# Gates' low-rank path moved beside the second group's recurrence, and a triangular inverse put together from 16x16 blocks, in a streaming-encoder trunk

## The chip, the cores and the metric

The kernel runs on one core of a Trainium2 chip. The metric is the device time of one execution in microseconds. The kernel before takes 1319.26 us, the median of 3 runs (1318.08 to 1319.82). One execution was recorded by the hardware profiler; all rows below come from it.

## The reference

The trunk has four residual layers on a 512 x 1024 activation (one batch): a spatial-gating MLP, a gated convolutional FFN, an RWKV-7 time mixer and a second FFN, each behind an RMS norm, and a last norm. Only the RWKV layer is changed:

```python
xx = token_shift(h) - h                      # h: 512 x 1024, already normed
xr, xw, xk, xv, xa, xg = (h + xx * mu[i] for i in range(6))
r, k, v = xr @ w_r, xk @ w_k, xv @ w_v
w = -softplus(-(w0 + tanh(xw @ w1) @ w2)) - 0.5      # w1: 1024 x 64
a = sigmoid(a0 + (xa @ a1) @ a2)                     # a1: 1024 x 64
g = sigmoid(xg @ g1) @ g2                            # g1: 1024 x 160, g2: 160 x 1024
...                                                  # kk from k; 16 heads of 64
y = wkv7_scan(r, exp(-exp(w)), k, v, -kk, kk * a)    # delta-rule state per head
y = groupnorm(y) * ln_w + ln_b + bonus               # bonus: sum(r*k*r_k) * v
return (y * g) @ w_o
```

The kernel doesn't step through 512 tokens. It cuts them into 8 chunks of 64; inside a chunk the recurrence becomes products of 64 x 64 matrices, one of which is the inverse of a unit triangular matrix per head and chunk.

## The kernel before, in words

**Layout and arithmetic.** Activations lie transposed: 8 k-tiles of 128 features by 512 tokens. Every large product is made in three parts from operands that are split into a high and a low half (`mm3`, L280: high·high, high·low, low·high). A split (`split`, L204) is a copy on ScalarE (the high half, L212) and a subtraction on VectorE or POOL (L213).

**The RWKV layer** has 16 heads in two groups of 8. It goes through these stages:

- `rwkv_first` (L621): low-rank products for decay and `a` on the incoming operand, not yet normed; the shift and the norm are made up for afterwards by `shifted` (L645), which needs `rb`, the norm's factor broadcast to all partitions (`rstd`, L313). Then the gate's low-rank products `ga` and `gb`, in the same way (weights scaled on VectorE, L371, then split; 72 parts of products), then the projection by `wra`, for which each k-tile is normed (L671), mixed (`mix`, L610: L612 on ScalarE, L613 on VectorE) and split into `mxh` and `mxl`. The gate's values go through tanh, are split and go out to memory (`sgd`). Last the projection by `wrb`.
- `pairs` (L915) with `projections` (L742): head pairs make the chunk matrices, while projections of k and v fill TensorE. `value` (L784) centres v (L790) and makes the bonus (L804). `invert(0)` (L942) runs beside the last pairs.
- `scan(0)` (L1036): the 8 chunks of group 0, each a chain of small products and copies (L1066, L1070, L1079, L1086, L1091), where the next chunk needs the state written by L1089. `vu` is the state and value operand, `us` and `e` are accumulators; L1081 is a copy on ScalarE that belongs to the chain. Beside it run the rest of the projections and `invert(1)`.
- `scan(1)` with `project` (L1144), the output projection by `wo`. `finish` (L1102) normalizes each pair of chunks (L1110 to L1120) and every second time gates the result (`mm3` and L1133 on 256 tokens, then L1135 to L1139). The gate values `sg` and weights `gw` are loaded at chunk 1 of each group (`gate_weights`, L1004).

**The inverse.** `invert` treats the 32 x 32 diagonal blocks of the 64 x 64 triangular matrices of a group, 128 of them, by forward substitution on VectorE: 31 steps of a multiplication (L970) and an addition (L971), then a transposition (L976). The two blocks of a matrix are put together by two products for each (L991, L994), in plain float32, which the trace shows as two passes each, addressed to 32 x 32 tiles of TensorE's array.

**What sets the order.** Programs are generators. `weave` (L1225) advances a main one (pairs or a scan), now and then a side one (the inverse), and a filling one (projections or the output projection) by rates in `RATES`; `LEAD` is a number of filling steps ahead of `scan(0)`. Each engine then works through its own queue in that order. Loads of weights are issued from ScalarE's queue (`wq`), loads of chunks and of the residual `h` from SP's.

Of the kernel before, what the change touches and what calls it, by code (L numbers as in the profile page):

```python
# [19 lines left out]
P = 128  # L20
# [10 lines left out]
RATES = ((1.9, 2), (1.9, 6, 2.2), (0.8, 2, 2), (0.7, 2), (2, 2), (0.7, 6, 2.2))  # L31
LEAD = 6
# [21 lines left out]
COFF = dict(ident=0, bones=128, center=256, masks=384, smask=512, causal=1024, blk2=1152, one=1154, id2=1155)  # L54
NCST = 1219


def constants():
# [13 lines left out]
    c[:, 1155:1219] = (i % C)[:, None] == np.arange(C)[None, :]  # L72
    return c


def layout(inp):
# [34 lines left out]
    a["g1a"] = g1[:, :, :P].reshape(P, 1024)  # L111
    a["g1b"] = np.concatenate([g1[:, :, P:], g1[:, :, P:]], axis=2).reshape(P, 512)
# [31 lines left out]
class Emit:  # L144
    def __init__(self, ctx, tc, A, out):
# [24 lines left out]
        self.wd = {n: [dp.tile([P, 2, 1024], F32, name=f"{n}d{m}") for m in range(KT)] for n in PARTS}  # L170
        self.n = self.turn = 0
# [69 lines left out]
    def make_parts(self, pool):  # L241

        nc = self.nc
        at = [(n, m, slice(c, c + 512)) for n in PARTS for m in range(KT) for c in (0, 512)]
        w = []
        for i in range(len(at) + 1):
            with self.tc.issue_after(self.last(mybir.EngineType.Activation)):
                if i < len(at):
                    n, m, c = at[i]
                    w.append(pool.tile([P, 512], F32, tag="pw", bufs=2, name=self.uid("pw")))  # L250
                    nc.sync.dma_start(w[i], self.A[n][m][:, c])
                if i:
                    n, m, c = at[i - 1]
                    for j, x in enumerate(self.split(pool, w[i - 1], [P, 512], "pw", bufs=1)):
                        nc.sync.dma_start(self.wd[n][m][:, j, c], x.bitcast(F32))
            yield

    def parts(self, n, m, whole):
# [13 lines left out]
        return 512, t  # L272

# [310 lines left out]
    def rwkv(self, gain):  # L584
        nc, tc, A = self.nc, self.tc, self.A
        V, S, G = nc.vector, nc.scalar, nc.gpsimd
        with ExitStack() as ctx:
# [7 lines left out]
            r.sgd = dp.tile([3, P, T], F32, name="sgd")  # L595
# [12 lines left out]
            def mix(i, k):  # L608
# [5 lines left out]
                return self.operand(t, lo_eng=(G, V)[k % 2])  # L614
# [6 lines left out]
    def rwkv_first(self, r, ep):  # L621
# [5 lines left out]
        r.sg = [ep.tile([P, T], F32R, name=f"sg{i}") for i in range(3)]  # L627

# [3 lines left out]
        def lowrank(n, w):  # L632
            a = self.acc()
            self.dense(a[0:n], w, hx, ncol=n)
            return a[0:n]
# [9 lines left out]
        def shifted(now, before, n):  # L645
            t, u = tmp("lt", 2), tmp("lu", 2, T + 1)
            G.memset(u[:, 0:1], 0.0)
            V.tensor_tensor(t[0:n], now, rb[0:n], ALU.mult)
            V.tensor_tensor(u[0:n, 1:], before, rb[0:n], ALU.mult)
            G.tensor_tensor(t[0:n], t[0:n], u[0:n, 0:T], ALU.add)  # L650
            return t
# [4 lines left out]
        S.activation(t[0:64], t[0:64], AF.Tanh)  # L656

        for j, x in enumerate(r.lr):
            hi, lo = slice(64 * j, 64 * j + 64), slice(64 - 64 * j, 128 - 64 * j)
            S.copy(x[hi], t[hi])  # L660
            V.tensor_tensor(x[lo], t[hi], x[hi].bitcast(F32), ALU.subtract)
# [4 lines left out]
        for kk in range(4):  # L666
            w = self.weights(A["wra"][kk])
            for j in range(2):
# [10 lines left out]
        for i, (x, n) in enumerate(((ga, P), ((gb[0:32], gb[32:64]), 32))):  # L679
            t = shifted(*x, n)[0:n]  # L680
            S.activation(t, t, AF.Tanh, scale=0.5)
            V.tensor_scalar(t, t, 0.5, 0.5, ALU.mult, ALU.add)
            if i == 0:
                S.copy(r.sg[0], t)
                V.tensor_tensor(r.sg[1], t, r.sg[0].bitcast(F32), ALU.subtract)
            else:
                self.stack(r.sg[2], t)
        for i, n in enumerate((P, P, 96)):
            nc.sync.dma_start(r.sgd[i, 0:n], r.sg[i][0:n].bitcast(F32))
# [13 lines left out]
    def rwkv_main(self, r, ctx, gain):  # L703
# [38 lines left out]
        def projections():  # L742

            load = Ahead([lambda n=n, m=m: self.parts(n, m, m % 3 == 2) for n in PARTS for m in range(KT)])
# [197 lines left out]
        def invert(g):  # L942
# [11 lines left out]
            pr = ip.tile([P, 272], F32, tag="pr", bufs=1, name=self.uid("pr"))  # L954
# [7 lines left out]
            V.transpose(li.rearrange("p s t -> p t s"), x.rearrange("p u t -> p t u"))  # L962
            for _ in range(WAIT):
                yield
            for j in range(31):
                ni, nj = 31 - j, j + 1
                a = li[:, j, j + 1:32].unsqueeze(1).to_broadcast([P, nj, ni])
                b = tt[:, 0:nj, j].unsqueeze(2).to_broadcast([P, nj, ni])
                q = pr[:, 0:ni * nj].rearrange("p (c i) -> p c i", i=ni)
                V.tensor_tensor(q, a, b, ALU.mult)  # L970
                V.tensor_tensor(tt[:, 0:nj, j + 1:32], tt[:, 0:nj, j + 1:32], q, ALU.add)  # L971
# [311 lines left out]
```

## Time and profile before

| what | value |
|---|---|
| median of 3 runs | 1319.26 us (1318.08 to 1319.82) |
| profiled execution | 1317.32 us, span 1315.5, mean granted clock 0.978 |
| `rwkv_first` | 519.35 to 593.88 us |
| pairs, projections, group 0's inverse | 593.88 to 772.32 us |
| `scan(0)`, group 1's inverse, the last projections | 772.32 to 839.19 us |
| `scan(1)`, output projection, the first products of the last FFN | 839.19 to 941.09 us |
| instructions | 19526 |

Times in rows are us from the start of the span. A row of the timeline has start, duration, engine, line, operation, output<-inputs, shape, count and, in brackets, idle time before it with what ended it. A matmul row's duration is longer than the distance to the next, since they are pipelined; the distance of starts is its cost in a row of many. The granted clock is a fraction of full speed.

### The profile page before, as it was taken

What the parts mean: (1) busy time and instruction counts of PE and PEld (TensorE: products, weight loads), DVE (VectorE), ACT (ScalarE), POOL (GpSimd) and SP (SyncE); (2) the same over time, 40 slices, a digit from 0 to 9 for tenths busy, and PEclk for the clock granted to TensorE, in tenths of its full rate; (3) what the DMA queues carried; (4) which work ended last, traced back from release to release, by engine and by line L of the source; (5) the groups of instructions that cost most, each with busy time, mean ns of one, the idle gap of its engine ahead of it and who ended that gap; (6) DMA issues with size and microseconds to landing.
All of it is one profiled execution on the core that took longest, in us unless ns stands there. A gap on an engine that the chain in (4) does not pass through costs nothing.

```text
span 1315.5 us, 19526 instructions
## 1 busy us (share of the span) xinstructions
PE 1272.7 (97%) x7618; PEld 1031.3 (78%) x7618; DVE 848.5 (64%) x1365; ACT 623.8 (47%) x1062; POOL 142.8 (11%) x152
## 2 busy tenths in 40 slices
PE   8999999999999999999999998898999999999996
PEld 6878888888888888787777766676888888888886
DVE  5565488788874444865869785656687777772223
ACT  5444455555554333565657644333554444442221
POOL 3100200000000010310111012332300000000001
PEclk9999999999999999999979996999999999999998
DMA  7332345555556753245877786881333232333322
GB/s 259 88 113 80 106 151 170 167 168 174 166 173 211 224 150 108 79 136 157 251 220 205 225 209 147 207 221 41 96 96 97 96 96 96 97 92 91 101 89 76
DMA packets 100461, 188.55 MB, mean 143 GB/s; under 512 B 16912, under 2 KB 47760, under 8 KB 100368
## 3 DMA queue, kind: packets, MB, share of 16 engines
q10 hardware_dynamic: 36448, 109.46, 27.2%
q1 hardware_dynamic: 63920, 77.84, 20.7%
q8 instruction: 60, 0.98, 0.3%
q14 instruction: 33, 0.27, 0.1%
HBM read 146.70 MB, written 40.57 MB: 142 GB/s over the span
## 4 chain that ended last, share of the span: by engine, by line
PE 78%; DVE 9%; ACT 3%; issue 2%; DMA 2%; POOL 1%; ACTq 0%; DVEq 0%; SPq 0%; POOLq 0%
PE mm L284 8%; PE mm L285 8%; PE mm L286 8%; PE e L284 5%; PE e L286 5%; PE e L285 5%; PE us L284 5%; PE us L286 5%; PE us L285 5%; PE aux L284 5%; PE aux L286 5%; PE aux L285 5%; DVE tt L971 1%; DVE pr L970 1%; PE us L1066 1%
## 5 line engine op out<-in xcount | busy, mean ns | idle before, releaser
L212 ACT CAST wh<-w 128x512 fp32r<-128x512 f32 (+1 forms) x361 | 220.1, 612 | 398.8 <-PE mm L285 97.1
L213 DVE TENSOR_TENSOR wl<-w,wh 128x512 fp32r<-128x512 f32 x353 | 243.8, 692 | 186.9 <-ACT wh L212 182.8
L284 PE MATMUL mm<-mxh,wh 128*128 128x512 f32 x392 | 161.2, 412 | 0.6 <-DVE h L1166 0.4
L285 PE MATMUL mm<-mxl,wh 128*128 128x512 f32 x392 | 155.7, 397 | 0.6 <-DVE mxl L1139 0.6
L286 PE MATMUL mm<-mxh,wl 128*128 128x512 f32 x392 | 155.9, 398 | 0.3 <-DVE wl L213 0.3
L311 POOL TENSOR_TENSOR ss<-ss,sq 128x512 f32<-128x512 f32 x30 | 40.7, 1357 | 777.3 <-issue 594.8
L284 PEld LDWEIGHTS mm<-mxh,wh 128*128 128x128 f32 x392 | 74.8, 191 | 20.1 <-issue 3.2
L507 ACT ACTIVATE cv<-z,par 128x512 f32<-128x512 f32 x88 | 71.7, 817 | 36.0 <-DVE z L505 35.9
L286 PEld LDWEIGHTS mm<-mxh,wl 128*128 128x128 f32 x392 | 74.7, 191 | 17.3 <-DVE wl L213 0.6
L285 PEld LDWEIGHTS mm<-mxl,wh 128*128 128x128 f32 x392 | 74.8, 191 | 16.3 <-DVE mxl L1139 1.3
L284 PE MATMUL e<-mxh,wh 128*128 128x512 f32 x216 | 84.5, 391 | 0.0
L284 PE MATMUL us<-mxh,wh 128*128 128x512 f32 (+1 forms) x216 | 84.4, 391 | 0.0
L286 PE MATMUL us<-mxh,wl 128*128 128x512 f32 (+1 forms) x216 | 84.1, 389 | 0.0
L285 PE MATMUL us<-mxl,wh 128*128 128x512 f32 (+1 forms) x216 | 84.1, 389 | 0.0
L285 PE MATMUL e<-mxl,wh 128*128 128x512 f32 x216 | 84.0, 389 | 0.0
L286 PE MATMUL e<-mxh,wl 128*128 128x512 f32 x216 | 84.0, 389 | 0.0
L508 DVE SCALAR_TENSOR_TENSOR cv<-z,par,cv 128x512 f32<-128x512 f32 x88 | 66.1, 752 | 23.9 <-ACT cv L507 23.9
L284 PE MATMUL aux<-mxh,wh 128*128 128x512 f32 x208 | 81.2, 391 | 0.2 <-ACT wh L212 0.2
L286 PE MATMUL aux<-mxh,wl 128*128 128x512 f32 x208 | 81.1, 390 | 0.0
L285 PE MATMUL aux<-mxl,wh 128*128 128x512 f32 x208 | 80.9, 389 | 0.0
L509 DVE SCALAR_TENSOR_TENSOR cv<-z,par,cv 128x512 f32<-128x512 f32 x88 | 66.0, 752 | 2.9
L284 PEld LDWEIGHTS e<-mxh,wh 128*128 128x128 f32 x216 | 40.6, 188 | 8.7 <-issue 0.5
(1071 smaller groups left out, 2679.4 us busy)
## 6 DMA issues: line engine op xcount, KB each, us to landing
w<-in_wup ACTq DMA_DIRECT2D x88, 512.0 KB, 3.5
w<-in_wdn ACTq DMA_DIRECT2D x32, 512.0 KB, 3.6
st<-std SPq DMA_DIRECT2D x32, 384.0 KB, 5.8
std<-lq SPq DMA_DIRECT2D x32, 256.0 KB, 4.6
w<-in_wdn ACTq DMA_DIRECT2D x16, 384.0 KB, 3.3
w<-in_wsu ACTq DMA_DIRECT2D x8, 512.0 KB, 3.5
w<-in_wso ACTq DMA_DIRECT2D x8, 512.0 KB, 3.5
pw<-in_wk SPq DMA_DIRECT2D x16, 256.0 KB, 3.9
```

The source lines that it names most:

```text
L212: nc.scalar.copy(hi[r, :n], src)
L213: (lo_eng or nc.vector).tensor_tensor(lo[r, :n], src, hi[r, :n].bitcast(F32), ALU.subtract)
L284: mm(acc, wh, xh, start=first, stop=False)
L285: mm(acc, wh, xl, start=False, stop=False)
L286: mm(acc, wl, xh, start=False, stop=last)
L311: nc.gpsimd.tensor_tensor(self.ss, self.ss, self.sq, ALU.add)
L507: nc.scalar.activation(c, z[:, 2:], AF.Identity, scale=cw(2, i), bias=self.p("conv_b", l * 44 + i))
L508: nc.vector.scalar_tensor_tensor(c, z[:, 1:T + 1], cw(1, i), c, ALU.mult, ALU.add)
L509: nc.vector.scalar_tensor_tensor(c, z[:, 0:T], cw(0, i), c, ALU.mult, ALU.add)
L970: V.tensor_tensor(q, a, b, ALU.mult)
L971: V.tensor_tensor(tt[:, 0:nj, j + 1:32], tt[:, 0:nj, j + 1:32], q, ALU.add)
L1066: nc.tensor.matmul(us[H[hd], 0, i, :], ar(i, hd, 0), vu[:, hd, i, :], start=True, stop=True)
```

## The change

Three things are done.

1. **The gate's low-rank path.** Its 72 partial products leave `rwkv_first`, with the scaling of weights, the shift and the trip to memory and back. A new generator `gates` runs in front of `project` as the filling work of `scan(1)`: it mixes and splits each k-tile of the normed input, multiplies by `g1` (48 partial products, 6 a k-tile), makes tanh and the splits, then gates all of group 0 in pieces of 512 tokens. The halves of `g1` are made beside the first FFN (`make_parts`) and lie in memory (`gd`). `h`, which `project` reloads with the residual, now stays the normed input until `gates` is through.
2. **The inverse.** Substitution goes down to 16 x 16 diagonal blocks: 15 steps, two blocks in one operation. Three rounds of products, 32 x 16 each (128, 64 and 128 of them in an inverse), put 32 x 32 blocks together; the 64 x 64 assembly stays.
3. **Order.** New `RATES`, `LEAD` 3 for 6; `scan(0)` no longer waits for the fourth `value` before it begins, but its loads do (`load`). In `rwkv_first` the norm's broadcast stands after 30 products instead of 48, with the low-rank results taken up after the second weight, and the mixes' low halves alternate between VectorE and POOL the other way round.

```diff
-RATES = ((1.9, 2), (1.9, 6, 2.2), (0.8, 2, 2), (0.7, 2), (2, 2), (0.7, 6, 2.2))
-LEAD = 6
+RATES = ((1.9, 2), (1.9, 6, 1.7), (0.65, 2, 1), (0.9, 2), (2, 2), (0.7, 6, 2))
+LEAD = 3
...
+        at += [(self.A["g1"], self.gd, slice(c, min(c + 512, 1280))) for c in (0, 512, 1024)]
...
-                return self.operand(t, lo_eng=(G, V)[k % 2])
+                return self.operand(t, lo_eng=(V, G)[k % 2])
...
-        lw = [lowrank(P, self.first)]
+        lw = [self.acc() for _ in range(2)]
+        self.dense(lw[0], self.first, hx[:4], last=False)
         norm = self.rstd()
         next(norm)
-        lw.append(lowrank(P, w))
+        self.dense(lw[0], self.first, hx[4:], first=False, c0=4 * P)
+        self.dense(lw[1], w, hx[:2], last=False)
         rb = next(norm)
+        self.dense(lw[1], w, hx[2:], first=False, c0=2 * P)
...
-        ga = [lowrank(P, self.lowrank_weights(A["g1a"], P, [f[:, :, 5]])) for f in (om, mu)]
-        gb = lowrank(64, self.lowrank_weights(A["g1b"], 64, [om[:, :, 5], mu[:, :, 5]]))
-        t = shifted(*lw, P)
...
+            if kk == 1:
+                lowrank()
...
-            for j in range(31):
-                ni, nj = 31 - j, j + 1
-                a = li[:, j, j + 1:32].unsqueeze(1).to_broadcast([P, nj, ni])
-                b = tt[:, 0:nj, j].unsqueeze(2).to_broadcast([P, nj, ni])
-                q = pr[:, 0:ni * nj].rearrange("p (c i) -> p c i", i=ni)
+            for j in range(15):
+                ni, nj = 15 - j, j + 1
+                a = diag(li, j, j + 1, [0, nj], [1, ni])
+                b = diag(tt, 0, j, [32, nj], [0, ni])
+                o = diag(tt, 0, j + 1, [32, nj], [1, ni])
+                q = pr[:, 0:2 * ni * nj].rearrange("p (d c i) -> p d c i", d=2, i=ni)
                 V.tensor_tensor(q, a, b, ALU.mult)
-                V.tensor_tensor(tt[:, 0:nj, j + 1:32], tt[:, 0:nj, j + 1:32], q, ALU.add)
+                V.tensor_tensor(o, o, q, ALU.add)
...
+            def small(out, lhs, rhs, rows):
+                for n in range(32):
+                    for r0 in rows:
+                        nc.tensor.matmul(out[r0, n, :], lhs(r0, n), rhs(r0, n), start=True, stop=True,
+                                         tile_position=(r0.start, r0.start))
...
+            small(q, lambda r0, n: tg[r0, n, col[r0.start]], lambda r0, n: z[r0, n, 0:16], quads)
+            V.tensor_tensor(w[:, :, 0:16], q, id4[:, :, 0:16].to_broadcast([P, 32, 16]), ALU.add)
+            yield
+            q = bank()
+            small(q, lambda r0, n: y[r0, n, :], lambda r0, n: w[r0, n, 0:16], firsts)
+            for r0 in firsts:
+                S.copy(z[r0, :, 0:16], q[r0])
+            yield
+            q = bank()
+            small(q, lambda r0, n: w[r0, n, :], lambda r0, n: y[r0, n, 16:32], quads)
+            S.copy(y[:, :, 16:32], q)
+            yield
...
+        def gates():
+            gw[0] = gate_weights(0)
+            ws = self.gate_parts()
+            yield
+            accs = [self.acc("mm")[0:n] for n in (P, 32)]
+            for k in range(KT):
...
+                    S.activation(t, self.hz[k][:, 0:T], AF.Copy, scale=self.p("mu", j))
+                    V.scalar_tensor_tensor(t, self.h[k], self.omu[:, j:j + 1], t, ALU.mult, ALU.add)
+                    x = self.operand(t)
+                for a, w, n in zip(accs, ws, (P, 32)):
+                    self.mm3(a, self.wcols(w, k * n, n), x, k == 0, k == KT - 1)
+                yield
...
+            while 0 not in normed:
+                yield
+            for i in range(4):
+                gate(0, i, slice(0, T))
+                yield
+            gated.add(0)
+            gw[1] = gate_weights(1)
...
         def load(g, c):
+            while 4 * g + 3 not in vdone:
+                next(fill)
...
-        while 3 not in vdone:
-            next(fill)
...
-        fill = project()
+        fill = itertools.chain(gates(), project())
```

The order in which an engine gets its work is not to be read from this. Three places follow; a row has a line, an operation, output<-inputs and a shape, with the line numbers of the kernel it stands in.

VectorE at the start of `rwkv_first`, before (`h_66` to `h_69` are k-tiles of the activation, `rb` the norm's broadcast, `w` and `wl` weights, `mt` a mix, `mxl` its low half):

```order
L213 TENSOR_TENSOR wl_4468<-w_861_4460,wh_4467 128x512
L213 TENSOR_TENSOR wl_4500<-w_867_4496,wh_4499 128x512
L371 TENSOR_TENSOR w_873_4532<-w_873_4532,omu 128x8x32
L371 TENSOR_TENSOR w_873_4532<-w_873_4532,par 128x8x32
L213 TENSOR_TENSOR wl_4504<-w_867_4496,wh_4503 128x512
L648 TENSOR_TENSOR lt_4565<-aux_4390,rb_4458 128x512
L649 TENSOR_TENSOR lu_4566<-us_4428,rb_4458 128x512
L671 SCALAR_TENSOR_TENSOR h_66<-h_66,par,rb_4458 128x512
L671 SCALAR_TENSOR_TENSOR h_67<-h_67,par,rb_4458 128x512
```

And with the change:

```order
L215 TENSOR_TENSOR wl_4488<-w_874_4485,wh_4487 128x512
L215 TENSOR_TENSOR wl_4492<-w_874_4485,wh_4491 128x512
L673 SCALAR_TENSOR_TENSOR h_66<-h_66,par,rb_4461 128x512
L673 SCALAR_TENSOR_TENSOR h_67<-h_67,par,rb_4461 128x512
L215 TENSOR_TENSOR wl_4540<-w_885_4537,wh_4539 128x512
L624 SCALAR_TENSOR_TENSOR mt_4497<-h_66,omu,mt_4497 128x512
L624 SCALAR_TENSOR_TENSOR mt_4518<-h_67,omu,mt_4518 128x512
L673 SCALAR_TENSOR_TENSOR h_68<-h_68,par,rb_4461 128x512
L215 TENSOR_TENSOR mxl_4501<-mt_4497,mxh_4500 128x512
```

The gate's weight scaling (L371) and the shift (L648, L649) no longer stand ahead of the normed k-tiles; the first mixes stand among the first weight splits.

TensorE in `scan(0)` where group 1's inverse is put together, before (L991 and L994 are the assembly of 64 x 64, L790 and L804 work of `value`, the others a chunk's chain):

```order
L804 MATMUL mm_7290<-rt_4363,wb_7288 128x512
L1086 MATMUL us_7114<-vu_6976,cbt_6975 64x64 x8
L1091 MATMUL e_7115<-vu_6976,st_6974 64x64 x8
L991 MATMUL aux_7218<-ix_7175,ti_5021 32x32 x32
L991 MATMUL aux_7253<-ix_7175,ti_5021 32x32 x32
L1066 MATMUL us_7302<-vu_7107,st_7105 64x64
L1070 MATMUL e_7303<-vu_7107,st_7105 64x64
L1066 MATMUL us_7302<-vu_7107,st_7105 64x64 x7
L1070 MATMUL e_7303<-vu_7107,st_7105 64x64 x7
```

With the change, a little earlier in the program (L987 is the new small product, L296 to L298 are `mm3`, L1145 to L1170 the chain):

```order
L987 MATMUL aux_7318<-ix_7282,ti_4913 32x16 x128
L785 MATMUL mm_7556<-cst,v_7286 128x128 x4
L1145 MATMUL us_7456<-vu_7222,st_7220 64x64
L1149 MATMUL e_7457<-vu_7222,st_7220 64x64
L296 MATMUL mm_7288<-mxh_5585,wh_7080 128x512
L1145 MATMUL us_7456<-vu_7222,st_7220 64x64 x7
L1149 MATMUL e_7457<-vu_7222,st_7220 64x64 x7
L1196 MATMUL aux_7479<-cst,y_7035 128x128 x4
L987 MATMUL aux_7488<-tt_7316,li_7283 32x16 x64
L297 MATMUL mm_7288<-mxl_5586,wh_7080 128x512
L298 MATMUL mm_7288<-mxh_5585,wl_7081 128x512
```

Between the chain's products now stand blocks of 128, 64 and 128 small products, and between these, parts of projections.

ScalarE in `scan(1)`, before, around the load of the gate's weights (L1011, L1012) and of an output weight (L237); L1081 and L1094 are copies of the chain:

```order
L1011 DMA w_1459_7820<-in_g 128x512
L1012 DMA w_1459_7820<-in_g 32x512
L237 DMA w_1470_7903<-in_wo 128x2x512
L212 CAST wh_7905<-w_1470_7903 128x512
L212 CAST wh_7909<-w_1470_7903 128x512
L1081 COPY vu_7743<-us_7831 64x256
```

With the change (L1160 and L1173 are the chain's copies, L1058 and L1061 the gate's tanh and split, L1086 the split of a gated piece, L239 the load of an output weight):

```order
L227 CAST sg_6966<-sq_8631 32x512
L1160 COPY vu_8511<-us_8606 64x256
L239 DMA w_1539_8777<-in_wo 128x2x512
L1086 CAST mxh_8659<-rt_4386 128x512
L1173 COPY y_8605<-e_8607 64x4x64 x2
L214 CAST wh_8779<-w_1539_8777 128x512
L214 CAST wh_8783<-w_1539_8777 128x512
L1086 CAST mxh_8690<-rt_4386 128x512
L214 CAST gwh_8771<-w_1535_8764 128x512
L1086 CAST mxh_8740<-rt_4386 128x512
L1160 COPY vu_8599<-us_8702 64x256
```

Before, the chain's copy (L1081) stands behind the load of an output weight and that weight's two splits. Now one copy of the chain stands ahead of that load, and the next stands behind three weight splits (L214) and three splits of gated pieces.

More of the change, by code (lines that the diff above doesn't have):

```diff
@@ L1 @@
+import itertools
 import math
@@ L742, in projections, with loads @@
         def projections():
-            load = Ahead([lambda n=n, m=m: self.parts(n, m, m % 3 == 2) for n in PARTS for m in range(KT)])
+            def loads(n, m):
+                return lambda: self.parts(n, m, m % 3 == 2)
+            load = Ahead([loads(n, m) for n in PARTS for m in range(KT)])
             def key(m, a):
@@ new lines, in gate @@
+        def gate(g, i, ts):
+            wh, wl, ws = gw[g]
+            c, n = slice(i * P, (i + 1) * P), ts.stop - ts.start
+            q = self.acc("aux")[:, 0:n]
+            self.mm3(q, (wh[:, c], wl[:, c]), [x[:, ts] for x in r.sg[0:2]], True, False)
+            nc.tensor.matmul(q, ws[0:96, c], r.sg[2][0:96, ts], start=False, stop=True)
+            o = rt[g][:, i, ts]
+            V.tensor_tensor(o, o, q, ALU.mult)
+            while len(outs[g]) <= i:
+                outs[g].append(tuple(self.xr.tile([P, T], F32R, tag=t, bufs=10, name=self.uid(t)) for t in ("mxh", "mxl")))
+            oh, ol = (x[:, ts] for x in outs[g][i])
+            S.copy(oh, o)
+            V.tensor_tensor(ol, o, oh.bitcast(F32), ALU.subtract)
@@ L1032, in load @@
             chunks[g, c] = st, bt, vu
-        left, sg = [], []
+        left = []
         def scan(g, late=iter(())):
@@ L1120, in finish @@
                 V.scalar_tensor_tensor(o, q[:, i * P:(i + 1) * P], self.p("ln_w", 4 * g + i), o, ALU.mult, ALU.add)
[L1121 to L1122 removed]
+            if b == 3:
+                normed.add(g)
+            if g == 1 and b % 2 == 1:
                 yield
[L1124 to L1139 removed]
+                while 1 not in gw:
+                    next(fill)
+                for i in range(4):
+                    gate(1, i, slice((b - 1) * P, (b + 1) * P))
+                    if i % 2 == 1 and b == 1:
+                        yield
                 if b == 3:
@@ L1198, in rwkv_main @@
         gw = {}
+        r.sg = [ep.tile([P, T], F32R, name=f"sg{i}") for i in range(3)]
         load(0, 0)
```

123 lines of the change are left out of this document (56 added, 67 removed).

## The prediction

> **What bounds the kernel now.** I read the page's busy times first, then the clock row, then a table of the four stages of the RWKV layer: first projections with the low-rank products; pairs with the rest of the projections and group 0's inverse; recurrence of group 0; recurrence of group 1 with the output projection. Columns: stretch, its us, busy us of each engine with instructions, granted clock, DMA share, GB/s.
>
> ```profile
> PE 1272.7 (97%) x7618; PEld 1031.3 (78%) x7618; DVE 848.5 (64%) x1365; ACT 623.8 (47%) x1062; POOL 142.8 (11%) x152
> PEclk9999999999999999999979996999999999999998
> ```
> ```profile
> core 0: us, PE busy (x) PEld busy (x) DVE busy (x) ACT busy (x) POOL busy (x), PEclk, DMA share, GB/s
> 519.35:593.88 74.53, 74.36 (x338) 59.99 (x337) 54.42 (x74) 42.83 (x74) 18.22 (x17) 1.00 0.33 106
> 593.88:772.32 178.44, 172.26 (x1407) 131.34 (x1405) 132.71 (x244) 113.62 (x213) 25.82 (x26) 0.95 0.75 213
> 772.32:839.19 66.87, 55.82 (x959) 45.67 (x958) 44.16 (x103) 28.52 (x58) 14.93 (x19) 0.82 0.75 178
> 839.19:941.09 101.90, 94.20 (x911) 73.88 (x909) 64.75 (x122) 40.31 (x84) 35.46 (x35) 0.95 0.52 137
> ```
> TensorE sets the time nearly everywhere. The first stage is solid work at full clock: what is removed there is gained. The other three idle 6.2, 11.1 and 7.7 us and run at 0.95, 0.82 and 0.95, which costs some 9, 12 and 5 us more; only there can added work hide. Next, where that idleness lies (stretches, then the waits: us in total, times, longest).
>
> ```profile
> 656.00:672.00 16.00, 15.35 (x93) 11.88 (x91) 9.93 (x19) 10.24 (x20) 2.07 (x3) 0.68 0.66 186
> 692.00:744.00 52.00, 49.31 (x412) 38.07 (x412) 49.44 (x108) 33.50 (x66) 6.63 (x4) 1.00 0.83 242
> 796.00:801.00 5.00, 0.61 (x16) 0.47 (x16) 4.87 (x10) 2.83 (x7) 2.92 (x3) 0.86 0.19 48
> 801.00:823.00 22.00, 20.53 (x436) 18.58 (x438) 8.12 (x17) 11.62 (x19) 3.55 (x5) 0.50 0.70 164
> 849.00:858.00 9.00, 7.20 (x44) 5.71 (x43) 4.75 (x10) 5.31 (x12) 2.51 (x3) 0.62 0.96 257
> 902.00:908.00 6.00, 3.34 (x26) 2.42 (x22) 3.44 (x5) 2.19 (x5) 2.86 (x2) 1.00 0.00 0
> 908.00:912.00 4.00, 3.60 (x19) 3.63 (x20) 2.67 (x7) 0.39 (x2) 0.00 (x0) 0.60 0.45 137
> ```
> ```profile
> PE aux L991 <- DVE ix L976: 6.3, 2, 4.7
> PE aux L1117 <- DVE y L1113: 3.5, 2, 3.1
> PE us L1086 <- ACT vu L1081: 1.7, 1, 1.7
> ```
> Group 1's inverse keeps TensorE waiting 4.7 us before 801, since VectorE (4.87 of 5 us busy) is late with the substitution; then the clock is 0.50 for 22 us although TensorE is busy for 20.53 of them. Group 0's substitution lies under projections, with VectorE busy 49.44 of 52.
>
> **First stage: 72 products out.** The gate's 72 products go, counted from the first of these rows to the second; the others feed the first mixed operand.
>
> ```profile
> 532.89 0.48 PE L284 MATMUL aux<-mxh,wh 128*128 128x512 f32 x1
> 549.41 0.39 PE L284 MATMUL mm<-mxh,wh 128*128 128x512 f32 x1
> 533.17 0.59 ACT L329 COPY rb<-mm 128x512 f32<-128x512 f32 x1 [0.50 <-PE mm L326]
> 535.00 2.44 DVE L671 SCALAR_TENSOR_TENSOR h<-h,par,rb 128x512 f32<-128x512 f32 x2
> 538.74 1.33 ACT L612 ACTIVATE mt<-h,par 128x512 f32<-128x512 f32 x2
> 540.17 1.41 DVE L613 SCALAR_TENSOR_TENSOR mt<-h,omu,mt 128x512 f32<-128x512 f32 x2
> 542.37 1.65 POOL L213 TENSOR_TENSOR mxl<-mt,mxh 128x512 fp32r<-128x512 f32 x1 [5.32 <-ACT mxh L212]
> ```
> ```profile
> L213 DVE TENSOR_TENSOR wl<-w,wh 128x512 fp32r<-128x512 f32 x353 | 243.8, 692 | 186.9 <-ACT wh L212 182.8
> ```
> 16.5 us over 72 is 0.229 us each. They covered the way from the norm's broadcast to the operand, 10.8 us from 533.17 to 544.0, much of it VectorE's queue. Now 18 products (4.1 us) stand behind the broadcast, and the way without queueing is 0.59 + 1.22 + 0.67 + 0.70 and a split of some 1.3: 4.5 us. Then each k-tile needs on VectorE 1.22 + 0.70 + one weight split and half an operand split of about 0.7 each, 3.0 us, against 12 products, 2.75 us. The stall is 0.5 us if only the first difference counts, 5 if the weight splits queue ahead as they do now. I take 3: −13.5 (−16 to −11.5). What takes the place of the gate's weight work here, three more pieces split in the FFN before, lies under that FFN's products (nines in the clock row); without that cover it would cost 3 × (0.6 + 0.7) = 3.9 us. The gates' three transfers out to memory and their way back fall away; two factor pairs read back later replace them.
>
> **Second stage: a shorter substitution, 320 products more.** The rows: weight loads of the inverse's present first product (at full and at half clock), the substitution's groups and two of its operations, and value work that leaves this stage.
>
> ```profile
> 743.35 1.09 PEld L991 LDWEIGHTS aux<-ix,ti 32*32 32x32 f32 x64 [1.85 <-DVE ix L976]
> 801.29 3.49 PEld L991 LDWEIGHTS aux<-ix,ti 32*32 32x32 f32 x128 [4.82 <-DVE ix L976]
> ```
> ```profile
> L971 DVE TENSOR_TENSOR tt<-tt,pr 128x31 f32<-128x31 f32 (+15 forms) x62 | 23.0, 370 | 1.4
> L970 DVE TENSOR_TENSOR pr<-li,tt 128x31 f32<-128x31 f32 (+15 forms) x62 | 22.2, 359 | 1.4
> ```
> ```profile
> 763.04 0.19 DVE L970 TENSOR_TENSOR pr<-li,tt 128x31 f32<-128x31 f32 x1
> 766.20 0.30 DVE L970 TENSOR_TENSOR pr<-li,tt 128x135 f32<-128x135 f32 x1
> 767.17 1.05 PE L790 MATMUL mm<-cst,v 128*128 128x128 f32 x8
> 769.90 1.10 PE L804 MATMUL mm<-rt,wb 128*128 128x512 f32 x2 [0.29 <-issue]
> ```
> One inverse has 62 operations now, 22.6 us of VectorE; with 30 of 0.19 to 0.30 us it takes about 7.5. TensorE pays: 320 products of two passes. A pass of L991 takes 1.09/64 = 17.0 ns at full clock, 3.49/128 = 27.3 ns at half. L991 alternates between two row tiles; 256 of the new products go round four, where two passes can overlap further: from 8.5 ns (half) to 17.0, and I take 12, near the middle. 512 × 12 + 128 × 17.0 = 8.3 us an inverse (6.5 to 10.9).
> The order lets 12 projection products (2.75), one centring and one bonus product (1.05, 1.10) slip behind this stage: −4.9. The first 1.6 us of the L991 waits goes (6.3 less 4.7), and VectorE's relief in 692 to 744 is worth part of 2.7 idle us: −2.5 together. A long run of tiny products may lower the clock, as 656 to 672 had 0.68 amid small ones: 0 to 6, I take +2. Around the products, the inverse also gains four clearings on POOL (26 of 178 us busy), one addition on VectorE and four copies on ScalarE. Each block of products waits for the copy or addition of the one before, so up to three times about 1 us could show; projections are there to fill it, and in the third stage chunks, so I count it at nothing, and three inverse steps at 1 us each are within the ends. In all −4.9 + 8.3 − 2.5 + 2 = +3 (−1 to +10).
>
> The Trainium skill, "TensorE: Matmul & The Clock Gate", section "Wait — 56ns, not 53.3ns?", says that matmuls never start closer than about 25 ns however small. By it 640 passes would be an estimated 16 us an inverse, and the whole sum about +10. The trace disagrees for this form: 17.0 ns.
>
> **Third stage: recurrence of group 0.** Chunk starts with nothing beside them (full clock, then half), and two successive gating blocks:
>
> ```profile
> 834.27 0.33 PE L1066 MATMUL us<-vu,st 128*64 128x64 f32 x2
> 839.19 0.34 PE L1066 MATMUL us<-vu,st 128*64 128x64 f32 x4
> 815.93 0.53 PE L1066 MATMUL us<-vu,st 128*64 128x64 f32 x4
> 822.13 0.53 PE L1066 MATMUL us<-vu,st 128*64 128x64 f32 x4
> 825.47 0.28 PE L1133 MATMUL aux<-sg,gw 96*128 96x256 f32 x1
> 825.96 0.28 PE L1133 MATMUL aux<-sg,gw 96*128 96x256 f32 x1
> ```
> Added: +4.9 slipped in, +8.3 for group 1's small products. Out: four of the eight gating blocks, each four products in 0.49 us: −2.0. The 4.7 us wait with its remainder of the 5 us stretch goes if the substitution is 15 us shorter: −5.1. At half clock 801 to 823 loses about 9 us (a chunk alone costs 6.2 there, 4.9 at full clock); more large products beside these chunks should return some, but the small ones are just the kind of work that ran at 0.50, so −5. Small products in the chain's waits: −2 of the 6 idle us left. In all −1 (−8 if the clock comes back whole, +10 if it doesn't and the products cost their upper end).
>
> **Fourth stage: gates beside group 1's recurrence.**
>
> ```profile
> 849.26 1.14 ACT L212 CAST wh<-w 128x512 fp32r<-128x512 f32 x2 [4.97 <-DMA w<-in_wo]
> ```
> 48 products at 0.229 come in, 11.0 us, and the gating of group 0 left over from stage 3, 2.0. Its operands come by eight mixes whose ScalarE and VectorE work (0.7 + 0.6 and 0.7 + 0.7 us a k-tile) fits beside engines busy 40 and 65 of 102 us. They cover: 902 to 912, where 3.1 idle us and about 1.4 of clock go, and 849 to 858, where ScalarE stands 4.97 us for an output weight with the chain's copy (L1081) queued behind it and TensorE waits 1.7 at L1086, with 3 of clock. That is 9 in reach; the weight's wait may recur, as the gate weights, the reload of the residual on SP's queue and the output weights now come later and closer together, with the chunks' own loads on SP. I take −7: +6 (0 with the chain's other waits covered too, to +11 if only 2 is covered).
>
> **Sum.** −13.5 + 3 − 1 + 6 = −5.5 against the profiled run, which took 1317.32 (span 1315.5 and 1.8 around it), 1.9 under the median; −5.5 from the median 1319.26 is 1314.
>
> **Rivals.** *Small products at low clock (slower).* One mechanism in both inverses: a hundred or more tiny passes in a row don't hold the clock, and they run between 17.0 and 27.3 ns, 22.2 on average: 14.2 us an inverse, +11.8 in all, and half of the clock gain of 801 to 823 stays out, +2.5. That is +9: 1328. For it: 0.50 with TensorE 93% busy, in just such work. Against: four row tiles, and 743.35 at full clock. It decides (slower by 0.2%) from 8.1 us over the forecast, which is 19.3 ns a pass on average. The skill's 25 ns lies beyond that.
> *Clock holds.* Passes at 8.5 ns (−3.6), no loss in stage two (−2), all 9 of 801 to 823 back (−4): −15, or 1304. For it: the 4.7 us wait just ahead of the low stretch is gone. Against: the stretch stayed at 0.50 long after it. The same page's "Part 1: The HAM clock gate" has the full clock back after some 3.4 us of sustained work, which would speak for this rival; the 22 us here don't agree.
> *Gates cost their whole length.* ScalarE's wait for a late weight returns in stage four with the chain's copy behind it: +11 there, sum −0.5, 1319, no change. For it: 4.97 at 849.26. Against: the gates' own products stand ready to run then.
>
> **How the numbers follow.** The forecast gets 0.36 (its own range 1308 to 1316.6), low clock 0.33, clock holds 0.16, gates at full price 0.15. A measurement can tell 0.2%, 2.6 us: faster is the forecast and the clock-holds case less a little at the edge, 0.50; same 0.15; slower 0.35. The terms' bounds add to −25 and +19.5; 1300 to 1332 leaves out the lower third of one outer case and the upper part of the other.
>
> **What would show it.** Stage one shorter by 11 to 16 us with full clock and VectorE near its bound; L991 no longer waiting for the substitution; small products at 12 ns a pass (over 19: the slow rival); the clock over the middle of group 0's recurrence above 0.5; group 1's recurrence with the gates between the chunks and no wait of 3 us at its end. I am wrong if the clock in either inverse sinks, if the first mixed operand is over 5 us late, or if ScalarE stands for a weight ahead of L1081's copy.

## The result: 38 us slower

The changed kernel takes 1356.79 us (median of 4 runs, 1352.98 to 1363.18) against 1318.67 (4 runs): 1.0297 times as long, 95% interval 1.025 to 1.0343. The forecast was 1314. The profiled execution took 1359.38 us, 42.1 more than that of before. Its page, with TensorE's busy time, the clock and one row of the part on DMA queues:

```profile
PE 1292.8 (95%) x8858; PEld 1040.8 (77%) x8858; DVE 829.0 (61%) x1309; ACT 636.2 (47%) x1080; POOL 143.9 (11%) x156
PEclk9999999999999999999796978899999999999998
q8 instruction: 69, 1.13, 0.4%
```

The same four stages as in the prediction, with the same columns:

```profile
519.42:581.12 61.70, 58.79 (x263) 46.74 (x262) 42.66 (x58) 36.15 (x62) 14.68 (x13) 1.00 0.29 95
581.12:777.21 196.09, 179.68 (x2029) 139.12 (x2027) 119.22 (x210) 114.48 (x213) 26.89 (x34) 0.91 0.66 182
777.21:862.63 85.42, 68.17 (x1604) 54.06 (x1605) 30.86 (x68) 31.43 (x63) 15.11 (x19) 0.82 0.62 148
862.63:983.00 120.37, 109.96 (x958) 80.37 (x957) 80.72 (x148) 54.22 (x105) 37.66 (x35) 0.96 0.51 135
```

They are 12.6 shorter, then 17.5, 18.5 and 18.5 us longer (stage one of before counted to 593.7, where its last product ends). TensorE's busy time grows in the last three, but it also idles 16.4, 17.3 and 10.4 us, where it idled 6.2, 11.1 and 7.7. The four of its waits there with the longest single ones, as before in us in total, times and longest:

```profile
PE aux L987 <- issue: 15.7, 6, 4.0
PE us L1158 <- DVE wt L1147: 7.0, 3, 6.6
PE mm L296 <- ACT mxh L214: 3.6, 2, 3.2
PE us L1145 <- DMA vu<-vtd: 2.6, 1, 2.6
```

L987 is the new small product. "issue" means that the profile shows nothing, no engine and no transfer of data, that TensorE waited for. The timeline of L987 in group 0's inverse, and at the end of group 1's:

```profile
714.28 1.53 PE L987 MATMUL aux<-ix,ti 32*32 32x16 f32 x161
719.85 1.48 PE L987 MATMUL aux<-ix,ti 32*32 32x16 f32 x95 [4.04 <-issue]
...
723.26 0.93 PE L987 MATMUL aux<-tt,li 32*32 32x16 f32 x28
726.20 2.85 PE L987 MATMUL aux<-tt,li 32*32 32x16 f32 x100 [2.01 <-issue]
...
734.37 2.29 PE L987 MATMUL aux<-li,tt 32*32 32x16 f32 x252
739.82 0.29 PE L987 MATMUL aux<-li,tt 32*32 32x16 f32 x4 [3.16 <-issue]
...
825.29 1.90 PE L987 MATMUL aux<-li,tt 32*32 32x16 f32 x128 [2.44 <-issue]
829.29 0.62 PE L987 MATMUL aux<-li,tt 32*32 32x16 f32 x30 [2.10 <-issue]
```

The passes themselves are quick, 252 in 2.29 us or 9 ns. Between the last two gaps stand exactly 128 passes. A pass is a weight load and a multiplication, so that is 256 instructions; and 128 passes of L987 and other products lie, three times over, between the restart at 726.20 and the gap before 739.82 (100, 16 large or centring ones, 16 of a pair's, 252). The queue named "instruction" on the page fits: 1.13 MB in 69 transfers are 16.4 KB each, for 8858 loads and 8858 multiplications 257 instructions a transfer. The page of before has, for 2 x 7618:

```profile
q8 instruction: 60, 0.98, 0.3%
```

254 a transfer. So TensorE's program seems to come in blocks of 256 instructions, and a block of small products (128 passes at 9 ns) is used up in about 1.2 us, faster than the next one comes. When each transfer landed isn't in the profile. That is the theory tested below, called supply. The Trainium skill, "Runtime: NRT & Kernel Launch", section "Instruction fetch mechanics", gives the same blocks of 256 instructions and says that the cost of passing from one to the next is mostly hidden; the trace agrees on the block and not on the cost, 15.7 us here.

The other rivals were the one on record that small products keep the clock low whatever feeds them, that the gates cost the time, and that the new order does.

### The profile page after: what moved, and what is told of

Read it like the earlier page. It is cut to its first block, busy times and chain, and to the rows that moved or that the text cites. A ratio compares the mean times of both kernels' runs of the same rounds, so it can differ in the third digit from the quotient of the medians.

```text
span 1357.6 us, 21984 instructions
## 1 busy us (share of the span) xinstructions
PE 1292.8 (95%) x8858; PEld 1040.8 (77%) x8858; DVE 829.0 (61%) x1309; ACT 636.2 (47%) x1080; POOL 143.9 (11%) x156
## 3 DMA queue, kind: packets, MB, share of 16 engines
q8 instruction: 69, 1.13, 0.4%
## 4 chain that ended last, share of the span: by engine, by line
PE 80%; DVE 7%; issue 4%; ACT 3%; DMA 1%; POOL 1%; ACTq 0%; DVEq 0%; SPq 0%; POOLq 0%
PE mm L296 8%; PE mm L297 8%; PE mm L298 8%; PE aux L297 5%; PE aux L296 5%; PE aux L298 5%; PE us L296 5%; PE us L297 5%; PE us L298 5%; PE e L296 5%; PE e L297 5%; PE e L298 5%; PE aux L987 1%; PE mm L785 1%; PE aux L903 1%
## 5 line engine op out<-in xcount | busy, mean ns | idle before, releaser
L214 ACT CAST wh<-w 128x512 fp32r<-128x512 f32 x356 | 216.9, 612 | 387.3 <-PE mm L297 105.9
L296 PE MATMUL mm<-mxh,wh 128*128 128x512 f32 (+1 forms) x384 | 160.9, 419 | 1.6 <-DVE h L1236 1.2
L297 PE MATMUL mm<-mxl,wh 128*128 128x512 f32 (+1 forms) x384 | 154.0, 401 | 0.0
L298 PE MATMUL mm<-mxh,wl 128*128 128x512 f32 (+1 forms) x384 | 153.5, 400 | 0.4 <-DVE wl L215 0.3
L296 PEld LDWEIGHTS mm<-mxh,wh 128*128 128x128 f32 (+1 forms) x384 | 73.6, 192 | 21.6 <-issue 4.0
L298 PEld LDWEIGHTS mm<-mxh,wl 128*128 128x128 f32 (+1 forms) x384 | 73.2, 191 | 18.3 <-issue 1.0
L297 PEld LDWEIGHTS mm<-mxl,wh 128*128 128x128 f32 (+1 forms) x384 | 73.6, 192 | 15.6 <-issue 1.5
L296 PE MATMUL e<-mxh,wh 128*128 128x512 f32 x216 | 84.5, 391 | 0.0
L298 PE MATMUL e<-mxh,wl 128*128 128x512 f32 x216 | 84.1, 389 | 0.0
L296 PE MATMUL aux<-mxh,wh 128*128 128x512 f32 x208 | 81.5, 392 | 0.2 <-ACT mxh L214 0.2
L296 PE MATMUL us<-mxh,wh 128*128 128x512 f32 x208 | 81.2, 391 | 0.0
L298 PE MATMUL aux<-mxh,wl 128*128 128x512 f32 x208 | 81.0, 389 | 0.0
L298 PE MATMUL us<-mxh,wl 128*128 128x512 f32 x208 | 81.0, 389 | 0.0
L297 PE MATMUL us<-mxl,wh 128*128 128x512 f32 x208 | 80.9, 389 | 0.0
L297 PEld LDWEIGHTS aux<-mxl,wh 128*128 128x128 f32 x208 | 39.1, 188 | 12.2 <-POOL mxl L215 2.7
```

The costliest lines, as they stand in the source:

```text
L214: nc.scalar.copy(hi[r, :n], src)
L296: mm(acc, wh, xh, start=first, stop=False)
L297: mm(acc, wh, xl, start=False, stop=False)
L298: mm(acc, wl, xh, start=False, stop=last)
```

## The experiments

Times are medians; each is compared with the kernel before in runs on the same chip (1317.1 to 1318.5 there).

### e1 and e2: one half of the change each

e1 is the kernel before with the changed `invert`, no other line; e2 the changed kernel with the old `invert` and

```diff
-RATES = ((1.9, 2), (1.9, 6, 1.7), (0.65, 2, 1), (0.9, 2), (2, 2), (0.7, 6, 2))
-LEAD = 3
+RATES = ((1.9, 2), (1.9, 6, 2.2), (0.8, 2, 2), (0.9, 2), (2, 2), (0.7, 6, 2.2))
+LEAD = 6
```

> The kernel before with only the 16x16 substitution and its small products; gates, rates and lead stay as before. Theory (supply): TensorE's instructions come in blocks of 256, and a block that is used up in less than some 4 us leaves it waiting, after which the clock is halved for a few us; so this kernel shows 10 us or more of 'issue' waits at the small products and is 15 to 35 us slower than before. Rival (gates): the loss comes from the gates and the new order, and the inverse alone changes -5 to +5 us.

> The changed kernel with the old 32x32 substitution, and the old rates and lead but for the second recurrence, so only the gates and group 0's gating have moved. Supply: no issue wait over 1 us in the inverses; first stage about -11, last stage +13 to +18, in all -3 to +10 us against before. Gates: +20 us or more.

e1 takes 1350.37 us, ratio 1.0253 (1.0229 to 1.0276): +32. e2 takes 1325.24, ratio 1.0059 (1.0029 to 1.0089): +7, with no issue wait over 0.6 us. The two add up to the change's 38. e1's first and last stages are as before (101.4 us the last); all of the loss is in the two stages that hold an inverse, whose issue waits at L993, the small product there, are 14.9 us:

```profile
593.20:791.06 197.86, 181.56 (x2048) 139.82 (x2046) 121.14 (x220) 116.18 (x218) 27.95 (x34) 0.92 0.69 192
791.06:873.50 82.44, 65.40 (x1599) 53.40 (x1598) 31.25 (x65) 31.09 (x62) 15.11 (x19) 0.81 0.61 146
```

e2 is a loss too, though the forecast's terms for the gates add to −9.5 (below).

### e4 and e7: as many columns in a fourth of the instructions

```diff
-                for n in range(32):
+                for n in range(0, 32, 4):
                     for r0 in rows:
-                        nc.tensor.matmul(out[r0, n, :], lhs(r0, n), rhs(r0, n), start=True, stop=True,
+                        nc.tensor.matmul(out[r0, n:n + 4, :], lhs(r0, n), rhs(r0, slice(n, n + 4)), start=True, stop=True,
```

e4 is the changed kernel so edited, e7 is e1.

> The changed kernel with one small product where it has four, each moving 64 columns instead of 16: as many columns in all, a fourth of the instructions (three of four blocks get the wrong factor, so the result of the inverse is not computed). Supply: no issue wait over 1 us at the small products, clock near 1 beside them, 15 to 30 us faster than the changed kernel. Low clock: the same array work on the same small tiles, at most 8 us faster.

> The kernel before with only the new inverse, as e1, and one small product where it has four, each moving 64 columns (the inverse's result is not computed): a fourth of the instructions for as many columns. Supply: e1's 32 us over before shrink to -5 to +8 us, no issue wait over 1 us at the small products. Rival (the products' place in the order and their waits for copies cost the time): at least 15 us over before.

e4: 1331.28 us, 25.5 less than the changed kernel; e7: 1325.25, 25.1 less than e1. The same 25 us in both. At the small products no issue wait is left in e4, and 1.5 us in e7 (none over 1 was expected). Stages two and three of e4:

```profile
581.50:762.44 180.94, 170.42 (x1550) 130.99 (x1548) 119.06 (x212) 114.39 (x213) 27.44 (x34) 0.95 0.72 197
762.44:831.94 69.50, 59.04 (x1124) 46.78 (x1125) 30.36 (x68) 31.50 (x64) 14.77 (x19) 0.88 0.73 176
```

15.2 and 15.9 us less than with all products: 31.1 in these two profiles, 25.5 in the medians. The issue waits at the small products, 15.7 us, are half of that. Most of the rest is the products' own time, since a fourth of the passes is less work for TensorE even with as many columns. The rows of the small products alone, in the changed kernel, in e4 and in e3 (below):

```profile
510.00:870.00 360.00, 18.13 (x1280) 16.92 (x1280) 0.91 0.59 158
510.00:870.00 360.00, 6.55 (x320) 5.58 (x320) 0.94 0.64 168
510.00:870.00 360.00, 17.99 (x1280) 15.92 (x1280) 0.92 0.60 162
```

Columns: stretch, its us, PE busy (x), PEld busy (x), clock, DMA share, GB/s. That is 11.6 us less in e4 (in e1 21.05, in e7 6.63). Part of the difference is the clock, 0.95 and 0.88 in the two stages where it was 0.91 and 0.82: after a gap TensorE comes back at half speed (95 passes in 1.48 us behind the gap at 719.85, 161 in 1.53 us ahead of it). So the 25 us of e4 and e7 are the supply's waits and the price of the passes together. The rival of the low clock needed 22.2 ns a pass on average; 18.13 us over 1280 passes are 14.2, and by this it falls. The 8 us that I allowed it here left out that fewer passes are less work. My "near 1" for the clock was too much: e4 keeps what else lowers it.

### e5: every small product twice

```diff
                 for n in range(32):
-                    for r0 in rows:
+                    for _ in range(2):
+                        for r0 in rows:
```

> The changed kernel with every small product issued twice, 640 more passes and 1280 more instructions in each inverse. Supply, with a block of 256 instructions every 4.0 us when TensorE waits for them: ten more blocks in the two inverses, 30 to 45 us slower than the changed kernel, with issue waits at the small products of 40 us or more, one after each 128 passes. Rival (array time, 8.4 to 17 ns a pass): 11 to 22 us slower.

1388.55 us, 31.8 more than the changed kernel, for 1280 passes: 25 ns each, where a pass takes 9 at full clock on four row tiles. The timeline, part of group 0's inverse:

```profile
712.73 1.53 PE L988 MATMUL aux<-ix,ti 32*32 32x16 f32 x161
717.59 1.90 PE L988 MATMUL aux<-ix,ti 32*32 32x16 f32 x128 [3.33 <-issue]
723.79 1.90 PE L988 MATMUL aux<-ix,ti 32*32 32x16 f32 x128 [4.29 <-issue]
727.51 1.48 PE L988 MATMUL aux<-ix,ti 32*32 32x16 f32 x95 [1.83 <-issue]
730.93 7.01 PE L988 MATMUL aux<-tt,li 32*32 32x16 f32 x256
...
748.80 1.91 PE L988 MATMUL aux<-li,tt 32*32 32x16 f32 x128 [3.15 <-issue]
752.26 1.91 PE L988 MATMUL aux<-li,tt 32*32 32x16 f32 x128 [1.55 <-issue]
755.99 0.29 PE L988 MATMUL aux<-li,tt 32*32 32x16 f32 x4 [1.82 <-issue]
```

128 passes, gap, 128 passes, gap. Restarts are 3.5 to 3.7 us apart, once 6.2; in the changed kernel 4.0 (825.29 to 829.29). Behind a gap the clock is 0.50 (717.59 to 721.00), and 128 passes take 1.90 us. The row at 730.93 explains why the issue waits are 27.9 us and not the 40 that I expected: this round goes over two row tiles instead of four, at half clock 128 of its passes take 3.5 us, as long as a block needs, and so no gap shows; the slow clock costs the time instead. Against the changed kernel's profile the issue waits grow by 12.2 us and the products' own time from 18.1 to 40.5. The time alone therefore doesn't decide against passes that merely run slow; what does is where the gaps fall, after 128 passes each.

### e3: the blocks cut into pieces

```diff
                 for n in range(32):
+                    if n and n % 8 == 0:
+                        yield
```

and the inverse's rate in group 0's recurrence 1.4 for 1, so that the pieces spread among chunks and projections.

> The changed kernel with its blocks of 128, 64 and 128 small products cut into pieces of 32 (16), so that filling products and chunks of the recurrence can stand between the pieces; side rate of the first recurrence 1.4 for 1. Supply: the issue waits at the small products fall from 15.7 to under 8 us, and the time by 8 to 20 us. Rival (low clock): small products run slow and keep the clock down however they are spread: within 5 us of the changed kernel.

1345.92 us, 10.9 less; issue waits at the products 4.2 us, as expected (6.3 with two at other products, against 16.1). The products are busy 18.0 us, as in the changed kernel, and so is TensorE as a whole in stages two and three (247.5 us, 247.9 there); it only idles 17.2 us less, in e3's fastest execution, the profiled one. 9.8 of them are issue waits. Most of the others are the 2.6 us for the first load, which are gone, and the 6.6 us for VectorE, of which 1.9 are left; what the other rate does by itself isn't shown. 14.6 us are left to e4, the larger part of it the 11.4 us that a fourth of the passes saves.

### e8: the rates of before on the changed kernel

The edit is e2's, without the old inverse.

> The changed kernel with the rates and the lead of before, but for the rate of the second recurrence. If the new order costs on its own (the first chunk waits 2.6 us for its load and 6.6 us for VectorE, which finishes the substitution first): 5 to 12 us faster than the changed kernel. If the products' instructions are all that counts: within 4 us of it.

1352.45 us, 4.3 less (ratio to before 1.0273, 1.0239 to 1.0307; the changed kernel's interval overlaps it). At the edge between the two: the wait for the load is gone in its profile and that for VectorE is 2.4 us, but the order is a small part at most.

### e6, e10, e11: feeding the gates

In the changed kernel the first product of the gates waits for its operand, and the clock is low behind it. Its row, and that stretch:

```profile
870.60 0.79 PE L296 MATMUL mm<-mxh,w 128*128 128x512 f32 x1 [3.23 <-ACT mxh L214]
868.00:884.00 16.00, 11.81 (x92) 6.76 (x92) 7.58 (x14) 3.93 (x7) 1.80 (x3) 0.68 0.49 103
```

e6 is e2 with each mix a step ahead; e10 is e2 with the inverse's rate in the first recurrence at 1; e11 is both, and two filling steps issued before the second recurrence:

```diff
         fill = itertools.chain(gates(), project())
+        next(fill)
+        next(fill)
```

> The kernel with the gates moved and the old inverse (e2), with each mix of the gates made one filling step before its products. If the 3.2 us wait of the first gate product for its operand, and the low clock behind it, are what the gates cost in the second recurrence: the wait goes and the time is 5 to 10 us under e2's 1325, about the time before. If the gates cost their products' length whatever feeds them: within 3 us of e2.

> The kernel with the gates moved and the old inverse (e2), with the same rate of 1 instead of 2. As in e9: 5 to 14 us less than e2's 1325 if the wait for the substitution is the cause of the low clock, under 5 us if not. A steadier clock would also narrow the spread of e2's times (1315 to 1334).

> As e10, and the gate weights' loads and the first mix are issued before the second recurrence begins, the later mixes one filling step ahead of their products. If the 3.2 us wait of the first gate product and the low clock behind it are a cost of the gates: the wait goes, the clock over the second and third chunk of that recurrence is above 0.95 (0.68 over 16 us in the changed kernel), and the time is 4 to 8 us under e10. If the gates cost their products' 11 us whatever feeds them: within 3 us of e10.

e6 takes 1321.88 us, 3.4 under e2 (the intervals of the two ratios overlap), but its wait is the same 3.2 us: its first mix starts only at 829.72 us, behind the first chunk's copies, so e6 doesn't test what it was made for. e10 takes 1323.41: the rate does little, and as in e9 below a wait for VectorE of 5.4 us has come in the place of the old one. In e11 the wait falls to 1.4 us, the clock is 0.93 over the second and third chunk (above 0.95 was expected), and it takes 1320.37, 3.0 under e10. That is at the border between the two expectations; the last stage is still 115.9 us in e11's profile, 14 longer than before.

### e9: the inverse's products two chunks later in the kernel before

```diff
-RATES = (..., (0.8, 2, 2), ...)
+RATES = (..., (0.8, 2, 1), ...)
```

> The kernel before with the inverse's rate in the first recurrence at 1 step for each step of the recurrence instead of 2, so that the products that put 64 x 64 together stand about two chunks later in TensorE's queue. If the half clock from 801 to 823 us follows from the 4.7 us in which TensorE waits for the substitution: the wait falls under 1 us, the clock there is above 0.8, and the time falls by 5 to 14 us. If small products alone bring the clock down: the low stretch only moves, and the time changes by less than 5 us.

1319.48 us, ratio 1.0019 (1.0004 to 1.0035): nothing gained. The 4.7 us wait of the inverse's product for VectorE is gone, and another has its place, since VectorE has the substitution in front of the chain's copy:

```profile
803.84 1.12 PE L1079 MATMUL us<-wt,ti 64*64 64x64 f32 x16 [5.08 <-DVE wt L1068]
```

From 801 to 823 us the clock is 0.77 where it was 0.50, short of the 0.8 that was expected. The experiment doesn't tell what lowers the clock, since its wait was only moved.

### e12 and e13: the gates' products in group 0's recurrence

`gates` is cut in two in e6: the low-rank products follow the projections as filling work of `scan(0)`, the gating stays in `scan(1)`.

```diff
+        fill = itertools.chain(fill, gates())
         load(0, 0)
...
-        fill = itertools.chain(gates(), project())
+        fill = itertools.chain(gating(), project())
```

The filling rate of that recurrence is 0.9, the inverse's 2 in e12 and 1.2 in e13. The filling rate of group 1's recurrence goes back from 0.9 to the 0.7 of before with it, so the place isn't the only difference from e6. The inverse is the old one.

> The kernel with the gates moved and the old inverse, with the gate's low-rank products (48, with their mixes one step ahead) as the filling work of group 0's recurrence, behind the last projections, and only the gating of group 0 in group 1's; filling rate of the first recurrence 0.9. If the gates cost their length in the second recurrence because TensorE has nothing to cover there (7.7 idle us of 102, as the first stage had none), and the first recurrence has (11 idle us of 67 and a clock of 0.82): the second recurrence falls from some 117 to about 104 us, the first grows by at most 5, and the time is 5 to 12 us under before. If work among the chunks costs its length anywhere: within 4 us of the kernel with the gates moved and mixes ahead (1322).

> As e12 with the inverse's rate in the first recurrence at 1.2 steps for each of the recurrence instead of 2. If where the inverse's products stand among the chunks matters, it differs from e12 by over 3 us; if not, by less.

e12 takes 1312.40 us, ratio to before 0.9948 (0.9929 to 0.9967), e13 1311.24, 0.9946 (0.9925 to 0.9966). Both beat the kernel before by 0.5%, as expected, and the changed one, which has the new inverse, by about 45 us. Stages three and four of e13:

```profile
758.31:828.82 70.51, 61.74 (x975) 44.39 (x974) 51.35 (x110) 38.00 (x72) 15.94 (x19) 0.93 0.69 165
828.82:932.04 103.22, 96.43 (x928) 75.41 (x925) 72.00 (x136) 43.84 (x89) 35.71 (x35) 0.93 0.61 160
```

The first recurrence takes in 11 us of gate products, gives up 2 of gating and grows by 3.6; the clock there is 0.93 where it was 0.82 before (0.89 in e2's profile). The second is back at 103. Between e12 and e13 there is no difference that can be measured.

## Why the prediction was wrong

| medians, us | old inverse | new inverse | new inverse, a fourth of the instructions |
|---|---|---|---|
| gates in the first stage | 1318.5 | 1350.4 | 1325.3 |
| gates in the second recurrence | 1325.2 | 1356.8 | 1331.3 |

Down the columns the gates cost 6 to 7, whichever the inverse. Along the rows the new inverse costs 32, of which 25 go with three of four small products.

- **First stage, −13.5.** Right: −12.6. TensorE waits for operands four times, for 0.21, 1.23, 0.68 and 0.72 us, 2.8 in all where 3 were taken.
- **Waits around the small products, counted at nothing.** This step failed. The price beside it held: 8.3 us an inverse were forecast, and TensorE is busy 9.4 and 8.8 us with them (9 ns a pass on four row tiles at full clock, 14.2 on average, where the sum has 13). The sum let the blocks wait for a copy or an addition only, with projections to fill that; what came is 15.7 us in which TensorE waits for no engine, at multiples of 128 passes, and a halved clock behind the gaps. The supply was in neither the sum nor a rival. The rows of before hold 64 or 128 such passes in a row, and the rate of instructions over a longer run can't be read from them. The rival of low clock had the sign and 1328, but not the mechanism: a pass took 14.2 ns on average and not 22.2, and the halved clock is a consequence here, as after the gaps at 719.85 and 726.20.
- **What the shorter substitution gives back, −2.5 and −5.1 with −5 of clock.** Failed for the most part. Without the small products the forecast for stages two and three is −5.3 and −9.3. e4, where the issue waits are gone, is 2.3 and 2.6 us over before in them, and without its 3.3 us of small products in each −1.0 and −0.7. So about 13 us that were counted on did not come. The 4.7 us wait for the substitution is gone, but in the changed kernel the chain's first copy stands behind it in VectorE's queue (the 6.6 us at L1158, 6.2 in e4), as in e9. At the end of stage two the first chunk waits 2.6 us for its load (L1145), which it does not with the old order in e8; the sum had neither. In e4's second stage TensorE also waits 3.0 us for the addition between two blocks, one of the steps put at nothing. In e13, where gate products stand there, no wait for VectorE in that recurrence is over 1.6 us.
- **Stages two and three together.** They are 36 us longer where +2 was forecast. An estimate from the profiles: 15.7 us of issue waits, 13 of gains that did not come, 1.5 of dearer passes; the 4 left are not traced one by one, and the half clock behind the gaps is the likely cause.
- **Last stage, +6.** Wrong by 12: +18.5, and +17.3 in e2. TensorE is busy 15.8 us more there, of which 13 were forecast; of the 7 us to be covered none were on balance. The 3.1 us wait near the end (L1117) is gone, as forecast, but the gates brought their own wait of 3.2 us with 16 us at 0.68. That is more than the rival of the whole length (+11) had, and not by its cause, a late weight: ScalarE waits 0.4 us for one. e11, which feeds the gates earlier, takes about 3 less. The place was at fault in the main, as far as the filling rate that e12 and e13 changed with it was not: the two recurrences together are 14.0 us over before in e2's profile, with the gates in the second, and 5.0 in e13's, with the 48 products in the first, where the trace had idle time and a low clock.
- **Range.** It ended at 1332. The unknown that I bounded was the price of a pass, between two rows of 64 and 128; the step from there to 256 and more in a row was taken for granted.

Some of the kernels spread more than others: e2 from 1315.5 to 1334.1, along with the granted clock from 0.986 to 0.971, e7, whose gates are not moved, from 1318.3 to 1330.7, e5 by 1.1 us only. e2's profile is of its fastest execution, so its stages add up to less than the 7 us of its median. What decides it from one execution to the next is open, as is what holds the clock at 0.50 from 801 to 823 us in group 0's recurrence of the kernel before.

## What to carry to other kernels

Count instructions as well as engine time: where a stretch of TensorE's program uses up 256 instructions in less than the 3.5 to 4 us that a block takes here, the block is the price, and fewer, wider products save twice: the waits, and the passes' own time. Work put beside a chain is hidden only where the profile shows TensorE idle or slow; 48 products cost more than their length in one recurrence and about half of it in the other. A wait that an engine's own queue causes moves with the order, so look what stands behind it before counting it as gained.

## What was not expected of the hardware

- TensorE's instructions came in transfers of 16.4 KB, 254 to 257 instructions each in all pages read (60 transfers before, 69 changed, 79 in e5). A run of small products stopped after 128 passes for up to 5.2 us (e1), with restarts mostly 3.5 to 4.0 us apart, and 6.2 (e5) and 6.5 (e1) at the longest.
- It isn't only the new products that run into it: TensorE waited 3.0 us for nothing that the profile shows at the assembly (L994) in e9, and 2.9 us at a product of the chain (L1110) in e7.
- A 32x16 pass took 9 ns on four row tiles at full clock and 15 at half, and 27 on two row tiles at half.
